# Strassen products for the second matrix product of two SwiGLU FFNs, with weight sums built in DRAM

## The chip, the cores and the metric

The kernel runs on one core of one Trainium2 chip. The metric is the device time of one execution in microseconds; several executions are timed and the median is given. A separate profiled execution supplies the trace. In the profile, PE is TensorE (PEld its weight loads), DVE is VectorE, ACT is ScalarE, POOL is GpSimd, and SP is SyncE, whose queue issues all DMAs of the kernel before.

## What is computed

One decoder layer in float32 on 512 tokens of width 1024. Four sublayers, each followed by a residual addition and a layer normalisation; the first and the last sublayer are SwiGLU FFNs with an inner width of 2816:

```python
def _swiglu(h, w_in, w_out):
    gate, up = jnp.split(h @ w_in, 2, axis=-1)
    return (jax.nn.silu(gate) * up) @ w_out

h = _layernorm(ALPHA * h + 0.5 * _swiglu(h, w_ffn1_in, w_ffn1_out), ln1_g, ln1_b)
h = _layernorm(ALPHA * h + _parallel_mixer(...), ln2_g, ln2_b)
h = _layernorm(ALPHA * h + _memory_attention(...), ln3_g, ln3_b)
h = _layernorm(ALPHA * h + 0.5 * _swiglu(h, w_ffn2_in, w_ffn2_out), ln4_g, ln4_b)
```

The change concerns the second product, `(silu(gate) * up) @ w_out`: 512 x 2816 times 2816 x 1024.

## The kernel before

All operands of the large matmuls are kept as two parts, a rounded high part and the rest (`split`, L64: a cast on ScalarE at L65, a subtraction on VectorE at L66). Each product of two 128-row tiles is three matmuls: high x high, high x low, low x high.

The code is written for a scheduler that fixes the order on each engine when the kernel is built, by operand readiness and by the order of the program, and inserts the semaphores. On the chip each engine then works through its own list in order: an instruction that waits holds up everything behind it on that engine. Buffers come from pools: `b8` has 13 slots of 8 KB a partition; `raw4` has 7 for weights as they arrive (512 KB a load); `q4` has 7 for their split parts. PSUM has 6 banks `mm` and 2 `tr`. A load is issued only when a raw buffer is free, that is when VectorE and ScalarE have read what stood in it.

*First product of an FFN* (`ffn`, L269). It yields the gated activations `gt`, six tiles that hold 22 blocks j of 128 inner columns, transposed. Blocks 0 and 1 are computed directly; the other 20 go two at a time through a Strassen-Winograd scheme: seven products (`a11`, `a12`, `s1`, `s2`, `s3`, `s4`, `a22`) of 12 matmuls of 256 columns each. For each j there is a load of the gate weights (`raw_f1g`, `raw_f2g`) and one of the up weights (`raw_f1u`, `raw_f2u`), both at L277. The sums of weights are made by VectorE at L301 to L304, beginning with `a21 - a22` at L301, which needs the up load. The loop at L367 runs over pairs `gi` = 0, 2, ... 18: products `s1` of the pair, `a22` of the pair before, `s4` and `s2` of the pair, the beginnings (`a12`, `a11`) of a later block, `s3` of the pair, another beginning. L336 subtracts the `s2` product from the gate; with that the PSUM bank of `s2` is read for the last time.

*Second product* (`out_gemm`, L193). For each of two halves of the 1024 output columns it runs over 11 weight blocks, each of 256 contraction rows x 512 columns (`wblock`, L69: a load at L71 and a split). For each block there are four row tiles t, two contraction tiles j and three matmuls of 512 columns:

```python
for i in range(head):
    w = wblock(wsrc[hf, order[i]], f"{name}{hf}_{i}")
    for t in range(NT):
        part(t, i, w)
```

The last blocks of a half (two in the first half, four in the second) are kept and run tile by tile, so that the addition into the residual `h[t]` (L227), the statistics (L230), the normalisation (`ln_tile`, L158) and, in the first FFN, the transposes of a row tile lie beside the matmuls of the next. The activations are split two contraction tiles at a time when they are first used (`act`, L389; 11 splits of 1024 elements).

Of the kernel before, what the change touches and what calls it, by code (L numbers as in the profile page):

```python
# [9 lines left out]
F32 = mybir.dt.float32  # L10
F32R = mybir.dt.float32r
I32 = mybir.dt.int32
AF = mybir.ActivationFunctionType
ALU = mybir.AluOpType
AX = mybir.AxisListType

P = 128
S = 512
D = 1024
KT = D // P  # L20
NT = S // P
FF = 2816
FT = FF // P
# [3 lines left out]
ALPHA = 2.0 ** 0.25  # L27
LN_EPS = 1e-5
# [5 lines left out]
def layer_kernel(ctx: ExitStack, tc: tile.TileContext, a, out):  # L34
    nc = tc.nc
# [3 lines left out]
    res = ctx.enter_context(tc.tile_pool(name="res", bufs=1))  # L39
    sm = ctx.enter_context(tc.tile_pool(name="sm", bufs=6))  # L40
    st = ctx.enter_context(tc.tile_pool(name="st", bufs=4))
    psum = ctx.enter_context(tc.tile_pool(name="psum", bufs=6, space=bass.MemoryType.PSUM))

    def b8(shape, dt, name):
        return big.tile(shape, dt, tag="b8", name=name)

    def mm_ps(name):
        return psum.tile([P, 512], F32, tag="mm", name=name)
# [15 lines left out]
    def split(src, hi, lo):  # L64
        nc.scalar.copy(out=hi, in_=src)  # L65
        nc.vector.tensor_tensor(out=lo, in0=src, in1=hi.bitcast(F32), op=ALU.subtract)  # L66


    def wblock(src, name, stay=False):  # L69
        raw = raw4([P, 1024], f"raw_{name}")  # L70
        nc.sync.dma_start(raw, src)  # L71
        if stay:
            both = b8([P, 2, 1024], F32R, f"ws_{name}")
            hi, lo = both[:, 0, :], both[:, 1, :]
        else:
            hi, lo = q4([P, 1024], f"whi_{name}"), q4([P, 1024], f"wlo_{name}")
        split(raw, hi, lo)
        return hi, lo
# [19 lines left out]
    for k in range(KT):  # L98
        x = xf[k // 4][:, k % 4, :]
# [3 lines left out]
        q = q4([P, 2, 512], f"qx{k}")  # L103
# [9 lines left out]
    def quarters_of(xT):  # L113

        return {n: [(x[:, sl], y[:, sl]) for x, y in xT[k0:k0 + 4]]
                for n, k0, sl in (("b11", 0, lo_), ("b21", 4, lo_), ("b22", 4, hi_))}
# [32 lines left out]
    h = [res.tile([P, D], F32, name=f"h{t}") for t in range(NT)]  # L149


    def ln_bcast(g, b):
        G, B = raw4([P, D], "G"), raw4([P, D], "B")
        nc.sync.dma_start(G, g.partition_broadcast(P))
        nc.sync.dma_start(B, b.partition_broadcast(P))
        return G, B

    def ln_tile(t, stats, GB, eps):  # L158
        G, B = GB
        mv = st.tile([P, 2], F32, tag="mv", name="mv")  # L160
# [32 lines left out]
    def out_gemm(wsrc, nkt, act, alpha, g, b, eps, name, final=False, order=None, stay=4, ys=None, pre=None):  # L193
        nb = nkt // 2
        order = list(range(nb)) if order is None else order
        tiles = None
        stats = [st.tile([P, 2, 6], F32, tag=f"stats{t}", name=f"stats{t}", bufs=1) for t in range(NT)]
        for hf in range(2):
            ps = [None] * NT
            head = nb - (2 if hf == 0 else stay)  # L200

            def part(t, i, w):
                if ps[t] is None:
                    ps[t] = mm_ps(f"{name}ps{hf}{t}")
                hi, lo = w
                for j in range(2):
                    ah, al = act(order[i] * 2 + j)
                    tsl = slice(t * P, (t + 1) * P)
                    wh, wl = hi[:, j * 512:(j + 1) * 512], lo[:, j * 512:(j + 1) * 512]
                    nc.tensor.matmul(ps[t], ah[:, tsl], wh, start=i == 0 and j == 0, stop=False)  # L210
                    nc.tensor.matmul(ps[t], ah[:, tsl], wl, start=False, stop=False)  # L211
                    nc.tensor.matmul(ps[t], al[:, tsl], wh, start=False, stop=i == nb - 1 and j == 1)  # L212
# [5 lines that stand above are left out]
            ws = [wblock(wsrc[hf, order[i]], f"{name}{hf}_{i}", stay=hf == 1 and i < head + 3) for i in range(head, nb)]  # L218
            if hf == 1:
                GB = ln_bcast(g, b)  # L220
                if pre is not None:
                    pre()
            for t in range(NT):
                for i, w in enumerate(ws):
                    part(t, head + i, w)
                sl = slice(hf * 512, hf * 512 + 512)
                nc.vector.scalar_tensor_tensor(  # L227
                    out=h[t][:, sl], in0=h[t][:, sl], scalar=float(alpha), in1=ps[t],
                    op0=ALU.mult, op1=ALU.add)
                nc.vector.bn_stats(stats[t][:, hf, :], h[t][:, sl])  # L230
                if hf == 1:
                    ln_tile(t, stats[t], GB, eps)
                    if final:
                        for q in range(2):
                            nc.sync.dma_start(out[t * P:(t + 1) * P, q * 512:(q + 1) * 512], h[t][:, q * 512:(q + 1) * 512])
                    else:
                        if t == 0:
                            tiles = [b8([P, 2, 2, S], F32R, f"{name}T{q}") for q in range(4)]
                        transpose_h(t, tiles, ys)
        if final:  # L240
            return None
        return [(tiles[k // 2][:, k % 2, 0, :], tiles[k // 2][:, k % 2, 1, :]) for k in range(KT)]


    def proj_T(w, X, n=S, name="pj"):
        hi, lo = w
        ps = mm_ps(name)
        for k in range(KT):
            wsl = slice(k * P, (k + 1) * P)
            mm3(ps[:, :n], hi[:, wsl], lo[:, wsl], X[k][0], X[k][1], k == 0, k == KT - 1)  # L250
        return ps[:, :n]
# [17 lines left out]
    def ffn(win, wout, xT, todo, g, b, name, final, first=None, lead=2, pre=None, ws0=None):  # L269
        gt = [b8([P, 4, S], F32, f"{name}g{q}") for q in range(-(-FT // 4))]  # L270
        raws, quads, ps, sg, c22 = {}, {}, {}, {}, {}
        X = quarters_of(xT)

        def load(j, u):
            if (j, u) not in raws:
                raws[j, u] = raw4([P, 1024], f"raw_{name}{'gu'[u]}{j}")
                nc.sync.dma_start(raws[j, u], win[u * FT + j])  # L277

        def quad(j, p):

# [25 lines left out]
        lo, hi = slice(0, 256), slice(256, 512)  # L306
# [49 lines left out]
        def begin(most):  # L356

            if len(begun) < len(order) and len(begun) - len(ended) < most:
                j = order[len(begun)]
                begun.append(j)  # L360
                product(j, "a12")
                product(j, "a11")
# [4 lines left out]
        for gi in range(0, len(order), 2):  # L367
            two = order[gi:gi + 2]
            for j in two:
                product(j, "s1")  # L370
            for j in order[max(gi - 2, 0):gi]:
                product(j, "a22")
                ended.append(j)
            for p in ("s4", "s2"):
                for j in two:
                    product(j, p)
            begin(4)
            for j in two:
                product(j, "s3")
            begin(4)  # L380
            if not final and 4 <= gi < 4 + 2 * NT:
                t = gi // 2 - 2
                nc.sync.dma_start(h[t], a["x"][t * P:(t + 1) * P, :])
        for j in order[-2:]:
            product(j, "a22")

        gs = {}

        def act(k):  # L389
            if k // 2 not in gs:  # L390
                T = gs[k // 2] = b8([P, 2, 2, S], F32R, f"{name}gs{k // 2}")
                split(gt[k // 4][:, k % 4:k % 4 + 2, :], T[:, :, 0, :], T[:, :, 1, :])
            T = gs[k // 2]
            return T[:, k % 2, 0, :], T[:, k % 2, 1, :]

        return out_gemm(wout, FT, act, 2.0 * ALPHA, g, b, 4.0 * LN_EPS, name, final, pre=pre)


    FQ, FF_, FG, FV = 0, 4, 8, 12
# [39 lines left out]
    for hd in range(H):  # L439
        pf = pf01[hd] if hd < 2 else proj_T(wblock(a["wmix"][FF_ + hd], f"wf{hd}"), X1, name="pf")  # L440
        sl = slice(hd * S, (hd + 1) * S)
# [11 lines left out]
    for hd in range(H):  # L453
        ps = tr_ps("dg")
# [366 lines left out]
```

## Time and profile before

| | |
|---|---|
| median of 3 runs | 1080.48 us (1080.31 to 1081.1) |
| profiled execution | 1082.22 us, of which the span of the trace is 1080.3 us |
| granted TensorE clock | 0.996 |
| busy: PE / VectorE / ScalarE / GpSimd | 1066.6 / 732.4 / 456.2 / 40.2 us |
| moved by DMA | 113.87 MB |
| first FFN: end of its first product | about 231 us |
| last FFN: first product, second product | about 732 to 953 us, 953 to 1073 us |

How to read rows of the profile: a group row gives line, engine, operation, output<-inputs with the shapes and a count, then the busy time of the group and the mean time of one in ns, then idle time of the engine before them and what ended it. A wait row gives who waited for whom, total us, times and longest. A timeline row begins with the start in us and a duration. A windows row gives a stretch, its length, busy time and count for PE, PEld, DVE, ACT and POOL, then the clock, the DMA share and GB/s.

### The profile page before, as it was taken

What the parts mean: (1) busy time and instruction counts of PE and PEld (TensorE: products, weight loads), DVE (VectorE), ACT (ScalarE), POOL (GpSimd) and SP (SyncE); (2) the same over time, 40 slices, a digit from 0 to 9 for tenths busy, and PEclk for the clock granted to TensorE, in tenths of its full rate; (3) what the DMA queues carried; (4) which work ended last, traced back from release to release, by engine and by line L of the source; (5) the groups of instructions that cost most, each with busy time, mean ns of one, the idle gap of its engine ahead of it and who ended that gap; (6) DMA issues with size and microseconds to landing.
All of it is one profiled execution on the core that took longest, in us unless ns stands there. A gap on an engine that the chain in (4) does not pass through costs nothing. (4 is left out here: it accounts for less than half of the span.)

```text
span 1080.3 us, 17019 instructions
## 1 busy us (share of the span) xinstructions
PE 1066.6 (99%) x6758; PEld 966.0 (89%) x6758; DVE 732.4 (68%) x1316; ACT 456.2 (42%) x810; POOL 40.2 (4%) x54
## 2 busy tenths in 40 slices
PE   9999999999999999999999999999999999999997
PEld 8899999998888888889889988888999999988885
DVE  7999878884425733675777456589987888882516
ACT  5666555572221332223415344335555555561300
POOL 0000000000000020411000000010000000000001
PEclk9999999999999999999999999999999999999999
DMA  9243233263341322222415521301323323443302
GB/s 359 72 136 100 89 111 114 80 188 105 106 139 56 99 62 91 71 80 79 156 39 195 153 82 40 128 29 59 118 79 118 118 79 117 135 124 98 133 1 78
DMA packets 34495, 113.87 MB, mean 105 GB/s; under 512 B 4336, under 2 KB 5616, under 8 KB 34416
## 3 DMA queue, kind: packets, MB, share of 16 engines
q1 hardware_dynamic: 34416, 112.78, 32.3%
q8 instruction: 53, 0.87, 0.3%
q14 instruction: 26, 0.21, 0.1%
HBM read 110.67 MB, written 2.10 MB: 104 GB/s over the span
## 5 line engine op out<-in xcount | busy, mean ns | idle before, releaser
L66 DVE TENSOR_TENSOR wlo_f<-raw_f,whi_f 128x1024 fp32r<-128x1024 f32 x38 | 46.5, 1223 | 85.7 <-PE f1ps L211 39.9
L65 ACT CAST whi_f<-raw_f 128x1024 fp32r<-128x1024 f32 x38 | 40.0, 1052 | 103.1 <-PE f2ps L212 46.5
L322 PE MATMUL f2u<-xt,qf2s 128*128 128x256 f32 x480 | 61.8, 284 | 0.7 <-DVE f2sg L336 0.7
L322 PE MATMUL f1u<-xt,qf1s 128*128 128x256 f32 x480 | 61.5, 284 | 0.0
L322 PEld LDWEIGHTS f2u<-xt,qf2s 128*128 128x128 f32 x480 | 59.1, 192 | 1.9 <-issue 1.9
L322 PEld LDWEIGHTS f1u<-xt,qf1s 128*128 128x128 f32 x480 | 59.4, 193 | 0.4 <-ACT qf1s L65 0.4
L210 PE MATMUL f1ps<-whi_f,f1gs 128*128 128x512 f32 x152 | 59.3, 390 | 0.0
L211 PE MATMUL f1ps<-wlo_f,f1gs 128*128 128x512 f32 x152 | 59.2, 389 | 0.0
L211 PE MATMUL f2ps<-wlo_f,f2gs 128*128 128x512 f32 x152 | 59.2, 389 | 0.0
L210 PE MATMUL f2ps<-whi_f,f2gs 128*128 128x512 f32 x152 | 59.1, 389 | 0.0
L212 PE MATMUL f1ps<-whi_f,f1gs 128*128 128x512 f32 x152 | 59.0, 391 | 0.0
L212 PE MATMUL f2ps<-whi_f,f2gs 128*128 128x512 f32 x152 | 58.8, 390 | 0.0
L165 POOL TENSOR_TENSOR rstd<-ve,mhalf 128x1 f32<-128x1 f32 x16 | 14.4, 900 | 685.4 <-DVE ve L163 685.4
L322 PE MATMUL f1v<-xT,qf1s 128*128 128x256 f32 x240 | 32.2, 291 | 2.1 <-ACT qf1s L65 2.1
L212 PEld LDWEIGHTS f2ps<-whi_f,f2gs 128*128 128x128 f32 x152 | 28.5, 188 | 6.1 <-DVE f2gs L66 0.3
L212 PEld LDWEIGHTS f1ps<-whi_f,f1gs 128*128 128x128 f32 x152 | 28.5, 188 | 6.0 <-DVE f1gs L66 0.3
L211 PEld LDWEIGHTS f2ps<-wlo_f,f2gs 128*128 128x128 f32 x152 | 28.5, 188 | 6.0
L210 PEld LDWEIGHTS f2ps<-whi_f,f2gs 128*128 128x128 f32 x152 | 28.5, 188 | 5.9
L211 PEld LDWEIGHTS f1ps<-wlo_f,f1gs 128*128 128x128 f32 x152 | 28.5, 188 | 5.9
L210 PEld LDWEIGHTS f1ps<-whi_f,f1gs 128*128 128x128 f32 x152 | 28.5, 188 | 5.8
L322 PEld LDWEIGHTS f1v<-xT,qf1s 128*128 128x128 f32 x240 | 30.8, 199 | 2.5 <-ACT qf1s L65 2.3
L322 PE MATMUL f1u<-xT,qf1a 128*128 128x256 f32 x240 | 32.1, 283 | 0.0
(337 smaller groups left out, 2957.1 us busy)
## 6 DMA issues: line engine op xcount, KB each, us to landing
raw_f<-in_w1out SPq DMA_DIRECT2D x22, 512.0 KB, 3.9
raw_f2g<-in_w2in SPq DMA_DIRECT2D x22, 512.0 KB, 3.8
raw_f2u<-in_w2in SPq DMA_DIRECT2D x22, 512.0 KB, 4.1
raw_f<-in_w2out SPq DMA_DIRECT2D x22, 512.0 KB, 3.7
raw_f1g<-in_w1in SPq DMA_DIRECT2D x20, 512.0 KB, 4.1
raw_f1u<-in_w1in SPq DMA_DIRECT2D x20, 512.0 KB, 4.4
raw_wk<-in_wk SPq DMA_DIRECT2D x8, 512.0 KB, 4.6
raw_mo<-in_wmixo SPq DMA_DIRECT2D x8, 512.0 KB, 3.6
```

Source lines behind the costliest of these rows:

```text
L65: nc.scalar.copy(out=hi, in_=src)
L66: nc.vector.tensor_tensor(out=lo, in0=src, in1=hi.bitcast(F32), op=ALU.subtract)
L165: nc.gpsimd.tensor_tensor(out=rstd, in0=ve, in1=mhalf[:, 0:1], op=ALU.pow)
L210: nc.tensor.matmul(ps[t], ah[:, tsl], wh, start=i == 0 and j == 0, stop=False)
L211: nc.tensor.matmul(ps[t], ah[:, tsl], wl, start=False, stop=False)
L212: nc.tensor.matmul(ps[t], al[:, tsl], wh, start=False, stop=i == nb - 1 and j == 1)
L322: nc.tensor.matmul(o, q[:, w, wsl], x[k][r], start=opens and k == 0 and n == 0, stop=ends and k == 3 and n == 2, skip_group_check=True)
```

## The change

Of the 22 contraction tiles of the second product, 16 (2048 rows) now go through one level of Strassen-Winograd; the other six go on as plain matmuls, tile by tile, at the end. The activations are cut into quarters `a11`, `a12`, `a21`, `a22` (256 tokens x 1024 inner columns), the weights into four quarters of 1024 rows x 512 columns. Seven products of 4 weight blocks x 2 x 2 x 3 matmuls of 512 columns replace eight. Left sums (`combine`) are made by VectorE in place in `gt`; left operands are split by `left`, two splits of 1024 elements a product; right operands are three quarters as they stand and four sums `t1` to `t4`. PSUM results are added into `h` by VectorE (`add`), eight additions during the Strassen part.

The sums `t1` to `t4` are built in DRAM during the first product of the same FFN. In the loop over pairs, from `gi` = 2 on, four copies of 512 KB from weight to scratch are issued on SP's queue, behind the up load of the pair's second block. With the fourth copy of a set, four accumulating DMAs are put on POOL's queue: t1 and t3 each add one weight block, t2 then adds t1, and t4 adds t2; each waits for what it reads and writes. Sixteen copies make four sets an FFN, at `gi` = 2, 4, 6 and 8. The new parts, cut to the core:

```diff
+    scr = ctx.enter_context(tc.tile_pool(name="scr", bufs=1, space=bass.MemoryType.DRAM))
...
+            for b in range(4):
+                for p, hf, kb in (("t1", 0, b), ("t3", 1, b), ("t2", 1, b + 4), ("t4", 0, b + 4)):
+                    self.todo.append((p, b, hf, kb))
...
+            for p, b, hf, kb in self.todo[:n]:
+                T = self.T[p, b] = scr.tile([P, 1024], F32, name=f"{self.name}{p}{b}")
+                with tc.issue_after(behind):
+                    nc.sync.dma_start(T, self.w[hf, kb])
+                if p == "t4":
+                    for o, x in (("t1", self.w[1, b]), ("t3", self.w[1, b + 4]), ("t2", self.T["t1", b]), ("t4", self.T["t2", b])):
+                        nc.gpsimd.dma_start(self.T[o, b], x, accum_op=ALU.add, max_dma_last_dim=8192)
+            del self.todo[:n]
...
+        u, v, w = ([mm_ps(f"{name}{n}{t}") for t in range(2)] for n in "uvw")
+        L = left("a11")
+        quarter_["s1"] = [x for x in [b8([P, 2, 4, 256], F32, f"{name}s1")] for x in (x[:, 0], x[:, 1])]
+        product(L, "b11", u, True, False)
+        combine("s1", "a21", "a22", ALU.subtract)
+        L = left("s1")
+        for t in range(2):
+            add(t, 0, u[t], True)
+        product(L, "t1", v, True, False)
+        combine("a21", "a11", "a21", ALU.subtract)
+        combine("a11", "s1", "a11", ALU.subtract)
...
+        product(L, "t2", u, False, False)
...
+        product(L, "b21", w, True, False)
+        combine("a12", "a12", "a11", ALU.add)
+        L = left("a21")
...
+        product(L, "t3", u, False, False)
...
+        product(L, "b22", v, False, False)
+        L = left("a22")
+        product(L, "t4", u, False, False)
+        ws = [[wblock(wsrc[hf, kb], f"{name}{hf}_{kb}", stay=hf == 0 or kb < 10) for kb in range(8, FT // 2)]
+              for hf in range(2)]
...
             begin(4)
+            if gi >= 2:
+                sums_out.copy(4, loads[two[-1]])
...
-        return out_gemm(wout, FT, act, 2.0 * ALPHA, g, b, 4.0 * LN_EPS, name, final, pre=pre)
+        return strassen_gemm(wout, gt, sums_out, 2.0 * ALPHA, g, b, 4.0 * LN_EPS, name, final, pre)
```

`product`, inside the new `strassen_gemm`, loads and splits four weight blocks (`right`, through `wblock`) and runs, for each, two contraction tiles x two row tiles x three matmuls into two PSUM banks:

```python
for i, (wh, wl) in enumerate(right(p)):
    for j in range(2):
        for t in range(2):
            for n, (x, y) in enumerate(((ah, wh), (ah, wl), (al, wh))):
                nc.tensor.matmul(ps[t], x, y[:, csl], ...)
```

The tail runs over the four row tiles; for each it takes both column halves with three blocks of weights each, then adds, takes statistics and normalises as before.

More of the change, by code (lines that the diff above doesn't have):

```diff
@@ L242, in out_gemm, with __init__, copy @@
         return [(tiles[k // 2][:, k % 2, 0, :], tiles[k // 2][:, k % 2, 1, :]) for k in range(KT)]
+    class Sums:
+        def __init__(self, wsrc, name):
+            self.w, self.name, self.T, self.todo = wsrc, name, {}, []
+            for b in range(4):
+                for p, hf, kb in (("t1", 0, b), ("t3", 1, b), ("t2", 1, b + 4), ("t4", 0, b + 4)):
+                    self.todo.append((p, b, hf, kb))
+        def copy(self, n, behind):
+            for p, b, hf, kb in self.todo[:n]:
[6 more added lines that the diff above has]
+            del self.todo[:n]
@@ new lines, in strassen_gemm, with left, combine, right @@
+    def strassen_gemm(wsrc, gt, S_, alpha, g, b, eps, name, final, pre):
+        tiles = None
+        stats = [st.tile([P, 2, 6], F32, tag=f"stats{t}", name=f"stats{t}", bufs=1) for t in range(NT)]
+        lo, hi = slice(0, 256), slice(256, 512)
+        quarter_ = {"a11": [gt[0][:, :, lo], gt[1][:, :, lo]], "a12": [gt[2][:, :, lo], gt[3][:, :, lo]],
+                    "a21": [gt[0][:, :, hi], gt[1][:, :, hi]], "a22": [gt[2][:, :, hi], gt[3][:, :, hi]]}
+        def left(p):
+            T = []
+            for i in range(2):
+                t = b8([P, 4, 2, 256], F32R, f"{name}{p}{i}")
+                split(quarter_[p][i], t[:, :, 0, :], t[:, :, 1, :])
+                T.append(t)
+            return T
+        def combine(o, x, y, op):
+            for i in range(2):
+                nc.vector.tensor_tensor(out=quarter_[o][i], in0=quarter_[x][i], in1=quarter_[y][i], op=op)
+        def right(p):
+            direct = {"b11": (0, 0), "b21": (0, 4), "b22": (1, 4)}
+            for i in range(4):
+                src = wsrc[direct[p][0], direct[p][1] + i] if p in direct else S_.T[p, i]
+                yield wblock(src, f"{name}{p}{i}")
+        def product(T, p, ps, opens, ends):
+            for i, (wh, wl) in enumerate(right(p)):
+                for j in range(2):
+                    k = 2 * i + j
+                    csl = slice(j * 512, (j + 1) * 512)
+                    for t in range(2):
+                        tsl = slice(t * P, (t + 1) * P)
+                        ah, al = T[k // 4][:, k % 4, 0, tsl], T[k // 4][:, k % 4, 1, tsl]
+                        for n, (x, y) in enumerate(((ah, wh), (ah, wl), (al, wh))):
+                            nc.tensor.matmul(ps[t], x, y[:, csl], start=opens and k == 0 and n == 0,
+                                             stop=ends and k == 7 and n == 2, skip_group_check=True)
+        def add(t, hf, ps, scale, op=ALU.add):
+            sl = slice(hf * 512, hf * 512 + 512)
+            if scale:
+                nc.vector.scalar_tensor_tensor(out=h[t][:, sl], in0=h[t][:, sl], scalar=float(alpha), in1=ps,
+                                               op0=ALU.mult, op1=op)
+            else:
+                nc.vector.tensor_tensor(out=h[t][:, sl], in0=h[t][:, sl], in1=ps, op=op)
+        u, v, w = ([mm_ps(f"{name}{n}{t}") for t in range(2)] for n in "uvw")
[4 more added lines that the diff above has]
+        L = left("s1")
+        for t in range(2):
+            add(t, 0, u[t], True)
+        product(L, "t1", v, True, False)
+        combine("a21", "a11", "a21", ALU.subtract)
+        combine("a11", "s1", "a11", ALU.subtract)
+        L = left("a11")
+        for t in range(2):
+            add(2 + t, 1, v[t], True)
+        product(L, "t2", u, False, False)
+        L = left("a12")
+        for t in range(2):
+            add(t, 1, u[t], True, ALU.subtract)
+        product(L, "b21", w, True, False)
+        combine("a12", "a12", "a11", ALU.add)
+        L = left("a21")
+        gs = {}
+        for k in range(16, FT, 2):
+            T = gs[k // 2] = b8([P, 2, 2, S], F32R, f"{name}gs{k // 2}")
+            split(gt[k // 4][:, k % 4:k % 4 + 2, :], T[:, :, 0, :], T[:, :, 1, :])
+        product(L, "t3", u, False, False)
+        L = left("a12")
+        for t in range(2):
+            add(2 + t, 1, u[t], False, ALU.subtract)
+        product(L, "b22", v, False, False)
[3 more added lines that the diff above has]
+              for hf in range(2)]
+        GB = ln_bcast(g, b)
+        if pre is not None:
+            pre()
+        for t in range(NT):
+            tsl = slice(t * P, (t + 1) * P)
+            for hf in range(2):
+                if t < 2:
+                    ps = (w, v)[hf][t]
+                else:
+                    ps = u[t - 2] if hf == 0 else mm_ps(f"{name}x{t}")
+                for i, (wh, wl) in enumerate(ws[hf]):
+                    for j in range(2):
+                        csl = slice(j * 512, (j + 1) * 512)
+                        ah, al = gs[8 + i][:, j, 0, tsl], gs[8 + i][:, j, 1, tsl]
+                        for n, (x, y) in enumerate(((ah, wh), (ah, wl), (al, wh))):
+                            nc.tensor.matmul(ps, x, y[:, csl], start=t >= 2 and hf == 1 and i == 0 and j == 0 and n == 0,
+                                             stop=i == 2 and j == 1 and n == 2, skip_group_check=True)
+                add(t, hf, ps, t >= 2 and hf == 0)
+                nc.vector.bn_stats(stats[t][:, hf, :], h[t][:, hf * 512:hf * 512 + 512])
+            ln_tile(t, stats[t], GB, eps)
+            if final:
+                for q in range(2):
+                    nc.sync.dma_start(out[t * P:(t + 1) * P, q * 512:(q + 1) * 512], h[t][:, q * 512:(q + 1) * 512])
+            else:
+                if t == 0:
+                    tiles = [b8([P, 2, 2, S], F32R, f"{name}T{q}") for q in range(4)]
+                transpose_h(t, tiles)
+        if final:
+            return None
+        return [(tiles[k // 2][:, k % 2, 0, :], tiles[k // 2][:, k % 2, 1, :]) for k in range(KT)]
@@ L271, in ffn @@
         raws, quads, ps, sg, c22 = {}, {}, {}, {}, {}
+        loads = {}
+        sums_out = Sums(wout, name)
         X = quarters_of(xT)
@@ L276, in load @@
                 raws[j, u] = raw4([P, 1024], f"raw_{name}{'gu'[u]}{j}")
-                nc.sync.dma_start(raws[j, u], win[u * FT + j])
+                loads[j] = nc.sync.dma_start(raws[j, u], win[u * FT + j]).ins
         def quad(j, p):
@@ L385, in ffn @@
             product(j, "a22")
[L387 to L394, printed above, removed]
-        return out_gemm(wout, FT, act, 2.0 * ALPHA, g, b, 4.0 * LN_EPS, name, final, pre=pre)
+        return strassen_gemm(wout, gt, sums_out, 2.0 * ALPHA, g, b, 4.0 * LN_EPS, name, final, pre)
     FQ, FF_, FG, FV = 0, 4, 8, 12
```

## The prediction

> **What bounds the kernel now.** I read the head of the page first (who is busy), then the DMA line, then windows over the stages that the change touches, then the waits.
>
> ```profile
> span 1080.3 us, 17019 instructions
> PE 1066.6 (99%) x6758; PEld 966.0 (89%) x6758; DVE 732.4 (68%) x1316; ACT 456.2 (42%) x810; POOL 40.2 (4%) x54
> GB/s 359 72 136 100 89 111 114 80 188 105 106 139 56 99 62 91 71 80 79 156 39 195 153 82 40 128 29 59 118 79 118 118 79 117 135 124 98 133 1 78
> ```
>
> PE is busy for all but 14 us, and most of those lie at the two ends. So matmuls that go away shorten the kernel, as long as nothing else becomes the last to arrive. The next fence is one answer of windows: the second product of the last FFN (953 to 1072), a stretch of its first product, and one of the first FFN's first product. The last columns are clock, DMA share and GB/s.
>
> ```profile
> 953.00:1072.00 119.00, 119.00 (x526) 98.32 (x525) 54.30 (x64) 28.23 (x29) 2.41 (x3) 1.00 0.24 76
> 774.00:794.00 20.00, 20.00 (x169) 20.00 (x169) 16.61 (x31) 11.31 (x23) 0.00 (x0) 1.00 0.34 107
> 82.00:102.00 20.00, 20.00 (x169) 20.00 (x168) 17.84 (x35) 12.31 (x24) 0.00 (x0) 1.00 0.34 106
> ```
>
> In the second product PE is never idle, at 119.00/526 = 0.226 us a matmul (512 columns); VectorE is used 46%, ScalarE 24%. In the first product VectorE is at 83 to 89%, and there it also waits for loads:
>
> ```profile
> DVE f2s L301 <- DMA raw_f2u<-in_w2in: 26.3, 16, 3.2
> DVE f1s L301 <- DMA raw_f1u<-in_w1in: 17.5, 13, 2.4
> PE f2u L322 <- DVE f2sg L336: 0.7, 2, 0.4
> ```
>
> VectorE loses 26.3 and 17.5 us to the loads of the second weight half ("up", u), and PE already loses 0.7 us because VectorE frees a PSUM bank late (L336). This stage has little room, and it is where the change puts its DMAs.
>
> **The change, part by part.** (1) *Matmuls.* Before, the 16 contraction tiles take 16 x 4 row tiles x 2 halves x 3 = 384 matmuls; after, 7 products x 4 blocks x 2 x 2 x 3 = 336, with the same 128x128 and 512-column shape. 48 fewer in each FFN, at 0.226 us: 10.85 us, 21.7 us for both. The six other tiles keep their 144.
>
> (2) *VectorE and ScalarE in the second product.* One subtraction of 1024 elements and one cast each:
>
> ```profile
> L66 DVE TENSOR_TENSOR f2gs<-f2g,f2gs 128x1024 fp32r<-128x1024 f32 x11 | 12.7, 1220 | 0.0
> L65 ACT CAST whi_f<-raw_f 128x1024 fp32r<-128x1024 f32 x38 | 40.0, 1052 | 103.1 <-PE f2ps L212 46.5 <-PE f1ps L212 46.3 <-issue 9.6
> L227 DVE SCALAR_TENSOR_TENSOR h<-h,f2ps 128x512 f32<-128x512 f32 x8 | 5.5, 686 | 19.8 <-PE f2ps L212 19.8
> ```
>
> VectorE gets 34 weight blocks to split in place of 22, 17 activation splits in place of 11, 8 sums of quarters (1024 elements, same form as the row above) and 8 more additions into h. That is 12 + 6 + 8 = 26 at 1.15 us (12.7/11, pipelined) = 30 us, plus 8 x 0.69 = 5.5 us: 54.3 + 35.5 = 90 us in a product that shrinks to about 108 us, 83%. The seven Strassen products alone: 28 + 14 + 8 + 3 of 1.15 us and 8 of 0.69 = 66.5 us, with 6 blocks of the rest in advance 73.4, beside 336 x 0.226 = 75.9 us of PE: 97%, of which some 3.5 us (first splits) fall before the first matmul. ScalarE has 51 casts of 1.05: 54 us. PE thus stays the longest, but barely. Price: from 0 (VectorE at 86% in the first product stalls PE for under 1 us) to about 10 us for each FFN (all the gain gone). I take 1.5 us each, 3 us together, since the first product is the nearest row. Behind the last matmul nothing changes: the same addition, statistics and normalisation.
>
> (3) *Loads of the second product.* 34 x 512 KB in 108 us instead of 22 in 119: 0.24 x (34/22) x (119/108) = 0.41 of the DMA engines. Cost nothing, covered by seven raw buffers; 16 of them read sums in DRAM that must be there.
>
> (4) *Copies and accumulations.* Each FFN gets 16 copies from DRAM to DRAM on SP's queue and 16 accumulations on POOL's, 512 KB each, in four sets. Set by set they follow the u loads of tiles 5, 7, 9 and 11. Here is SP's queue there, and what a DMA takes (KB, us to landing):
>
> ```profile
> 789.44 7.02 SPq L277 DMA_DIRECT2D raw_f2u<-in_w2in  x2
> 797.34 12.65 SPq L277 DMA_DIRECT2D raw_f2g<-in_w2in  x2
> 811.05 5.90 SPq L277 DMA_DIRECT2D raw_f2u<-in_w2in  x2
> 94.02 3.76 SPq L277 DMA_DIRECT2D raw_f1u<-in_w1in  x2
> 113.37 5.83 SPq L277 DMA_DIRECT2D raw_f1u<-in_w1in  x2
> raw_f2u<-in_w2in SPq DMA_DIRECT2D x22, 512.0 KB, 4.1
> h<-in_x SPq DMA_DIRECT2D x4, 512.0 KB, 10.8
> out<-h SPq DMA_DIRECT2D x8, 256.0 KB, 2.0
> L277 SPq DMA_DIRECT2D raw_f2g<-in_w2in x9: 328/328/328, 775.7 to 859.6; - x9
> ```
>
> Issuing a copy costs SP 0.33 us, where SP waits for buffers anyway. A period of two tiles is 20.16 us of PE (168 matmuls of 0.12), with four loads: 0.34 x 20.16 / 4 = 1.7 us of all engines for 512 KB. By the page's best slice (359 GB/s) it is 1.46 us. Writing to DRAM is no slower than reading (out lands in 2.0 us). So a set's four copies need about 6 us. An accumulation reads both operands: between one and two times a load, 1.7 to 3.4 us. A period's DMA work becomes 6 + 6 + 6 to 13 = 18 to 25 us of 20.16: full or nearly. The sums have time: the fourth set is issued near 817, its first reader stands at 953 + 11 = 964. POOL has nothing else in this stretch but a memset that sits in its queue until a buffer comes free:
>
> ```profile
> POOL pl L493 <- DVE qf1s L66: 213.5, 2, 212.0
> ```
>
> Were accumulations queued behind it, they would still end before the first FFN's second sub-product, some 240.
>
> What counts is whether a transfer meets a load that is waited for. The gate loads (g) at 797.34 stand behind the copies and land some 6 us later. An earlier one, of 775.66, is cast only at 795.40:
>
> ```profile
> 775.66 12.59 SPq L277 DMA_DIRECT2D raw_f2g<-in_w2in  x2
> 795.40 0.62 ACT L65 CAST qf2a<-raw_f2g 128x512 fp32r<-128x512 f32 x1
> ```
>
> With 4 us to land, 15 us are spare, so these cost nothing. The u loads are the ones without room:
>
> ```profile
> 794.81 0.69 DVE L301 TENSOR_TENSOR f2s<-raw_f2u 128x512 f32<-128x512 f32 x1 [2.06 <-DMA raw_f2u<-in_w2in]
> 799.91 0.69 DVE L301 TENSOR_TENSOR f2s<-raw_f2u 128x512 f32<-128x512 f32 x1 [1.06 <-DMA raw_f2u<-in_w2in]
> 782.53 0.42 DVE L336 TENSOR_TENSOR f2sg<-f2sg,f2u 128x256 f32<-128x256 f32 x1
> 786.29 3.04 PE L322 MATMUL f2u<-xt,qf2s 128*128 128x256 f32 x24
> 804.46 0.41 DVE L336 TENSOR_TENSOR f2sg<-f2sg,f2u 128x256 f32<-128x256 f32 x1
> 806.45 3.04 PE L322 MATMUL f2u<-xt,qf2s 128*128 128x256 f32 x24
> 106.46 0.41 DVE L336 TENSOR_TENSOR f1sg<-f1sg,f1u 128x256 f32<-128x256 f32 x1
> 110.22 3.04 PE L322 MATMUL f1u<-xt,qf1s 128*128 128x256 f32 x24
> ```
>
> VectorE's queue stands at L301 until the u load lands; L336, which frees the bank for PE, is behind it. L336 ends 3.3 us before PE needs it at 786, 1.6 us at 806, and PE waits for it by 888. VectorE's loop, from u load to u load, is thus longer than PE's 20.16 (789.44 to 811.05 is 21.6). So in the last FFN a delay of d at each of 8 u loads costs 8d. In the first FFN the loop is 19.35 (94.02 to 113.37), 0.8 us a period to spare over four periods, and L336 is 3.35 us early at 110, of which I count 2.4: 8d - 5.6, not below 0.
>
> d lies between 0 (never together) and 3.4 us (a whole accumulation in front of each). Copies issued at 796.5 are done by about 804, before the u loads of 811. Accumulations follow one another in the chain t1, t2, t4, each 1.7 to 3.4 of transfer and 2.4 of landing (4.1 - 1.7): about 800 to 818. So the u loads of 811.05 and 816.62 each meet one for part of their transfer. I take d = 1 us: 8 us in the last FFN, 2.4 us in the first.
>
> The Trainium skill's page "Collectives: The Full Stack", section "The bandwidth ceiling: the fold count and why AG ≠ RS ≠ AR", says that an add in the DMA path runs at half a copy's rate, since both operands are read through one ring. By that the accumulation stands at the upper end above, and a sum with d = 2 would give 29 - 21.7 = 8 us slower in place of the gain below; no run here shows an accumulating DMA yet.
>
> **Sum.** -21.7 + 3 (VectorE) + 8 + 2.4 (late u loads) = -8.3 us. The profiled execution took 1082.2 us (span 1080.3); it would become 1073.9. The median of the runs is 1080.5, 1.7 below: I predict 1072.2.
>
> **Rivals.** *The DMAs stay hidden* (d from 0 to 0.3): cost 3 to 5.4 us, time 1062 to 1064. For it: engines are two thirds idle and only part of each u load can meet an accumulation. Against: the work of a period fills it. *The DMA engines are saturated, slower than before* (place: L301 in the first products): accumulations at 3.4 us run into the next set's copies, and every u load waits for one. With d = 2.5: 20 + 14.4 + 3 - 21.7 = +15.7, 1096. The sum is zero where 16d - 5.6 + 3 = 21.7, at d = 1.5; above that the change loses. For it: 18 to 25 us of work in 20.16, and two PSUM waits that exist already. Against: the copies are issued right after the u loads, not before them. Beside this stands the Trainium skill's "DMA: Bandwidth & Descriptors", section "Issuing engines are not separate DMA queues": issuing from POOL gives no other engines, all interleave on the same 16. That agrees with this rival's mechanism; of POOL's queue this trace has no DMA to show. *VectorE becomes the bound of the second product*: 97% use with waits at each sum of quarters costs 5 us a FFN, 10 in place of 3: 1079, no change. *The saving does not appear* because the remaining matmuls run slower: excluded, they have the same shape and a new 128x128 weight load each, as now (PEld 98 of 119 us).
>
> **How the numbers follow.** My case (d from 0.4 to 1.4, 1065 to 1079): 0.41. Hidden: 0.21. Saturated: 0.26. VectorE bound: 0.12. About 0.2% (2.2 us) is what a measurement of this kernel can tell from no change. Faster: 0.38 of the first, all of the hidden case and a little of the last, 0.60. Same: 0.12. Slower: 0.28, the saturated case and what VectorE adds if both come. The range of 8 in 10 goes from 1060 (d = 0, VectorE nearly free) to 1094 (d about 2.4); the first case's own range is 1065 to 1079.
>
> **What would show it.** Right: 480 matmuls in place of 528 between the last L322 and the last normalisation of each FFN, in some 110 us without PE gaps over 1 us; the waits of L301 for u loads up by 5 to 10 us in each FFN; PE waiting for L336 for some 8 us in the last FFN's first product and little in the first's; u loads of tiles 6 to 13 landing about 1 us later than 4.1. Wrong: u loads landing in 6 us or more, PE waits for L336 over 15 us (saturated); no new wait there (hidden); or PE waiting in the second product for weight or activation splits of L66 (VectorE bound). The prediction is also wrong if SP itself stands behind the copies, so that u loads are issued late rather than land late.

## The result, and the profile after

The changed kernel took 1095.49 us in the median of four runs (1091.77 to 1098.38), beside 1080.79 us for the kernel before: 1.0133 times as long, 95% interval 1.0100 to 1.0166. It is slower by 14.7 us, where 8.3 us less were forecast. The profiled execution was the fastest of the four, 1091.77 us, with a span of 1090.0 us, so it shows 9.7 us of the loss.

From the page of the changed kernel: the head, the granted clock and the DMA share in 40 slices, and the two queues with their packets, MB and share of 16 engines.

```profile
span 1090.0 us, 17139 instructions
PE 1055.6 (97%) x6662; PEld 957.1 (88%) x6662; DVE 799.5 (73%) x1384; ACT 490.4 (45%) x846; POOL 65.8 (6%) x86
PEclk9999999999999999999999999999998899999999
DMA  9599823345680322212416421412998433256622
q1 hardware_dynamic: 38896, 142.15, 38.8%
q0 software_dynamic: 2560, 16.78, 8.2%
```

The 96 matmuls are gone (6758 to 6662) and PE has 11 us less to do, yet it is busy 97% instead of 99%. In the slices of the two first products (the first nine, and slices 28 to 36) the DMA row reaches 8 and 9, and two slices of PEclk read 8.

Windows over the four stages show where the time went: first and second product of the first FFN, then of the last FFN. The columns are the stretch, its length, busy time of PE, weight loads, VectorE, ScalarE and POOL, then clock, DMA share and GB/s. A first product is counted from the first L322 matmul of its Strassen part to the last, so blocks 0 and 1 lie ahead of it; in the first FFN of before it ends at 234.2 us, not near 231. First the kernel before, then the changed one:

```profile
27.80:234.20 206.40, 204.31 (x1682) 203.45 (x1682) 177.31 (x326) 120.59 (x228) 0.53 (x6) 0.99 0.34 110
234.20:357.20 123.00, 122.99 (x555) 101.36 (x554) 60.25 (x76) 35.39 (x43) 2.94 (x3) 1.00 0.31 97
748.80:953.00 204.20, 203.49 (x1682) 202.21 (x1682) 170.86 (x316) 113.69 (x221) 0.00 (x0) 1.00 0.34 109
953.00:1072.80 119.80, 119.79 (x528) 98.65 (x526) 54.30 (x64) 28.23 (x29) 2.41 (x3) 1.00 0.24 78
```

```profile
26.80:244.70 217.90, 209.18 (x1682) 206.83 (x1682) 176.91 (x326) 119.57 (x228) 13.17 (x22) 0.98 0.61 184
244.70:358.40 113.70, 112.79 (x507) 92.25 (x506) 94.90 (x113) 53.20 (x62) 2.96 (x3) 1.00 0.49 160
750.20:972.50 222.30, 209.51 (x1682) 208.75 (x1682) 170.58 (x316) 113.73 (x221) 12.53 (x16) 0.96 0.60 176
972.50:1082.50 110.00, 109.19 (x481) 89.73 (x479) 88.25 (x99) 45.90 (x47) 2.77 (x3) 1.00 0.44 144
```

The second products became 9.3 and 9.8 us shorter. The first products, with the same 1682 matmuls, became 11.5 and 18.1 us longer. That is +29.6 - 19.1 = +10.5 us, and 0.8 us less elsewhere makes the 9.7. The growth has two parts. PE's idle time (length minus busy) rose from 2.1 to 8.7 and from 0.7 to 12.8 us, 18.7 in sum; its busy time for the same matmuls rose by 4.9 and 6.0 us, 10.9 in sum, at a clock of 0.98 and 0.96. The second part is told with the hardware below.

The waits of the changed kernel (us in total, times, longest) and its DMA issues over the whole span (count, KB each, median us to landing):

```profile
DVE f2s L436 <- DMA raw_f2u<-in_w2in: 44.5, 16, 8.3
DVE f1s L436 <- DMA raw_f1u<-in_w1in: 31.5, 15, 6.0
L457 PE MATMUL f2u<-xt,qf2s 128*128 128x256 f32 x480 | 67.3, 301 | 12.8 <-DVE f2sg L471 11.1
L457 PE MATMUL f1u<-xt,qf1s 128*128 128x256 f32 x480 | 65.4, 293 | 6.7 <-DVE f1sg L471 6.0
f2t<-in_w2out SPq DMA_DIRECT2D x16, 512.0 KB, 8.3
f2t<-in_w2out POOLq DMA_DIRECT2D x8, 512.0 KB, 8.6
f2t<-f2t POOLq DMA_DIRECT2D x8, 512.0 KB, 7.6
```

L436, L457 and L471 are L301, L322 and L336 of before. VectorE waits for the u loads 44.5 and 31.5 us, where it was 26.3 and 17.5, and PE in turn waits for VectorE's L471 11.1 and 6.0 us, where it was 0.7 in the last FFN. The next fence has the same DMA view for the four periods of the last FFN alone (785 to 868 us): the DMA share in 40 slices and the u loads, first before, then after, and last the u loads of the first FFN (70 to 145 us), before and after.

```profile
DMA  0185028500006813840000771294000068119400
raw_f2u<-in_w2in SPq DMA_DIRECT2D x8, 512.0 KB, 4.1
DMA  9999999579999998999266999699989805991000
raw_f2u<-in_w2in SPq DMA_DIRECT2D x6, 512.0 KB, 6.8
raw_f1u<-in_w1in SPq DMA_DIRECT2D x8, 512.0 KB, 4.3
raw_f1u<-in_w1in SPq DMA_DIRECT2D x7, 512.0 KB, 6.3
```

The engines had pauses before and have almost none after. The u loads land 2.7 and 2.0 us later in the median.

One set from issue to end, from the timelines of SP, POOL, VectorE and PE (start us, length, engine, line, operation, count, idle time before it and what ended it):

```profile
802.58 2.61 SPq L259 DMA_DIRECT2D f2t<-in_w2out  x4
811.54 0.77 POOL L262 DMA_DIRECT2D f2t<-in_w2out  x1 [8.05 <-DMA f2t<-in_w2out]
815.84 12.28 SPq L412 DMA_DIRECT2D raw_f2u<-in_w2in  x2
826.47 0.69 DVE L436 TENSOR_TENSOR f2s<-raw_f2u 128x512 f32<-128x512 f32 x1 [8.34 <-DMA raw_f2u<-in_w2in]
826.67 0.78 POOL L262 DMA_DIRECT2D f2t<-f2t  x1 [7.05 <-DMA f2t<-f2t]
838.59 5.46 PE L457 MATMUL f2u<-xt,qf2s 128*128 128x256 f32 x24 [5.00 <-DVE f2sg L471]
```

Four copies go out from 802.58, the first accumulations at 811.54, the last at 826.67; that one lands 5.5 us later, at 832.2. The set takes some 30 us, longer than the 20 us period, and the last accumulation of the set before it goes out at 802.72, beside these copies. The u load issued at 815.84 in the midst of it starts VectorE only at 826.47, 10.6 us later, and PE then stands 5.00 us until 838.59.

### The profile page after: what moved, and what is told of

Same layout as the page of the kernel before. It is cut to its first block, busy times and chain, and to the rows that moved or that the text cites. A ratio compares the mean times of both kernels' runs of the same rounds, so it can differ in the third digit from the quotient of the medians.

```text
span 1090.0 us, 17139 instructions
## 1 busy us (share of the span) xinstructions
PE 1055.6 (97%) x6662; PEld 957.1 (88%) x6662; DVE 799.5 (73%) x1384; ACT 490.4 (45%) x846; POOL 65.8 (6%) x86
## 3 DMA queue, kind: packets, MB, share of 16 engines
q1 hardware_dynamic: 38896, 142.15, 38.8%
## 5 line engine op out<-in xcount | busy, mean ns | idle before, releaser
L457 PE MATMUL f2u<-xt,qf2s 128*128 128x256 f32 x480 | 67.3, 301 | 12.8 <-DVE f2sg L471 11.1
L457 PEld LDWEIGHTS f2u<-xt,qf2s 128*128 128x128 f32 x480 | 65.0, 210 | 13.5 <-issue 11.6
L457 PE MATMUL f1u<-xt,qf1s 128*128 128x256 f32 x480 | 65.4, 293 | 6.7 <-DVE f1sg L471 6.0
L457 PEld LDWEIGHTS f1u<-xt,qf1s 128*128 128x128 f32 x480 | 62.0, 200 | 8.6 <-issue 7.2
L436 DVE TENSOR_TENSOR f2s<-raw_f2u 128x512 f32<-128x512 f32 x20 | 13.8, 691 | 44.6 <-DMA raw_f2u<-in_w2in 44.5
L436 DVE TENSOR_TENSOR f1s<-raw_f1u 128x512 f32<-128x512 f32 x20 | 13.7, 691 | 31.5 <-DMA raw_f1u<-in_w1in 31.5
L457 PE MATMUL f1v<-xT,qf1s 128*128 128x256 f32 x240 | 32.2, 291 | 2.1 <-ACT qf1s L66 2.1
L457 PEld LDWEIGHTS f1v<-xT,qf1s 128*128 128x128 f32 x240 | 31.0, 200 | 2.5 <-ACT qf1s L66 2.3
L457 PE MATMUL f2w<-xoT,qf2a 128*128 128x256 f32 x240 | 32.8, 287 | 0.0
L457 PE MATMUL f1w<-xT,qf1a 128*128 128x256 f32 x240 | 32.2, 284 | 0.0
L457 PE MATMUL f2u<-xoT,qf2a 128*128 128x256 f32 x240 | 32.0, 283 | 0.0
L457 PE MATMUL f1u<-xT,qf1a 128*128 128x256 f32 x240 | 32.0, 283 | 0.0
L457 PEld LDWEIGHTS f2w<-xoT,qf2a 128*128 128x128 f32 x240 | 31.2, 197 | 0.1
L457 PEld LDWEIGHTS f1w<-xT,qf1a 128*128 128x128 f32 x240 | 30.6, 193 | 0.1
L67 DVE TENSOR_TENSOR wlo_wv<-raw_wv,whi_wv 128x1024 fp32r<-128x1024 f32 x12 | 14.7, 1224 | 21.5 <-PE vps L603 12.6
L457 PE MATMUL f1u<-xt,qf1a 128*128 128x256 f32 x240 | 30.4, 283 | 0.0
L457 PE MATMUL f2v<-xt,qf2s 128*128 128x256 f32 x240 | 30.4, 283 | 0.0
L457 PE MATMUL f2v<-xoT,qf2s 128*128 128x256 f32 x240 | 30.4, 283 | 0.0
L457 PE MATMUL f2u<-xt,qf2a 128*128 128x256 f32 x240 | 30.4, 283 | 0.0
L457 PE MATMUL f1v<-xt,qf1s 128*128 128x256 f32 x240 | 30.4, 283 | 0.0
L457 PEld LDWEIGHTS f1u<-xT,qf1a 128*128 128x128 f32 x240 | 30.2, 192 | 0.0
```

The lines of the kernel that those rows point to most:

```text
L436: nc.vector.tensor_tensor(out=s1, in0=a21, in1=a22, op=ALU.subtract)
L457: nc.tensor.matmul(o, q[:, w, wsl], x[k][r], start=opens and k == 0 and n == 0, stop=ends and k == 3 and n == 2, skip_group_check=True)
```

## The experiments

The theory: the accumulating DMAs fill the 16 engines, the u loads land late, VectorE stops at L436 and PE at the bank that L471 frees. The rivals: the copies, not the accumulations; instructions, waits and queue order, not bytes; or the second product itself.

**e1: Strassen with no sums at all.** Copies and accumulations are left out, and the operands of t1 to t4 are plain weight blocks, as many loads as before.

```diff
...
-            if gi >= 2:
-                sums_out.copy(4, loads[two[-1]])
```

> Strassen second products without any copy or accumulation; their right operands t1 to t4 are plain weight blocks, so the sums of weights are left out. Theory A (the DMA engines are full in four periods of each first product, so loads of up weights land late): first products return to the 206 and 204 us of before, second products stay at 114 and 110 us, time near 1080.8 - 9.3 - 9.9 = 1061.6. Theory B (the new order of instructions, not the DMAs, makes the first products longer): they stay at about 218 and 222 us, time near 1093. Theory C (Strassen itself stalls VectorE): second products over 115 us.

1061.73 us, 0.9834 of before (0.9816 to 0.9851). Its stages, the first product of the first FFN, then the first and second product of the last:

```profile
27.91:234.27 206.36, 204.27 (x1682) 203.45 (x1681) 177.31 (x326) 120.44 (x228) 0.53 (x6) 0.99 0.35 111
739.60:941.79 202.19, 202.19 (x1682) 201.91 (x1681) 170.94 (x316) 114.01 (x221) 0.00 (x0) 1.00 0.34 110
941.60:1051.70 110.10, 109.32 (x482) 89.86 (x480) 88.31 (x98) 46.07 (x47) 2.41 (x3) 1.00 0.45 145
```

The second product is as long as in the changed kernel (110.1 and 110.0 us), and the loss of both first products is gone (206.4 and 202.2 us, beside 206.4 and 204.2 before). So the second product isn't to blame: Strassen there is worth 18.5 us, and making the sums costs 33.8 us.

**e2: the copies alone.** No accumulation is issued; the operands are the bare copies.

```diff
-                if p == "t4":
-                    for o, x in (("t1", self.w[1, b]), ...):
-                        nc.gpsimd.dma_start(self.T[o, b], x, accum_op=ALU.add, ...)
```

> The 16 copies of each FFN stay, the 16 accumulations go (the sums of weights are left out, the products read the copies). Theory A with the work of both kinds counting: DMA share of the four periods about 0.33 + 4.4/20 = 0.55, up loads at 4 to 5 us, first products within 3 us of before, time 1062 to 1068. Theory A2 (the copies, which are long and stand in the queue of the loads, do the harm): first products stay over 212 us each, time over 1080.

1061.31 us, 0.9827 (0.9812 to 0.9843), the same as e1. A stretch of its first product, then its waits:

```profile
774.00:794.00 20.00, 20.00 (x169) 20.00 (x168) 16.17 (x30) 10.76 (x21) 0.00 (x0) 1.00 0.53 183
DVE f2s L433 <- DMA raw_f2u<-in_w2in: 25.3, 17, 3.0
```

Sixteen more DMAs of 512 KB in each FFN cost nothing that can be seen, and in this trace each set of them has landed before the next pair of u loads is issued. The DMA share rises to 0.53; VectorE's waits for u loads in the last FFN are as before, in the first FFN 20.2 us beside 17.5.

**e3: plain copies in place of the accumulations.** Same queue, same waits, same bytes written, but the second operand isn't added; the sums are left out.

```diff
-  nc.gpsimd.dma_start(self.T[o, b], x, accum_op=ALU.add, max_dma_last_dim=8192)
+  nc.gpsimd.dma_start(self.T[o, b], x, max_dma_last_dim=8192)
```

> The accumulations become plain copies on the same queue, with the same waits, descriptors and destinations, and without the second read (the sums are left out). If the bytes read twice are what fills the engines (accumulation about 2.8 us of all engines against 1.1 of a copy): DMA share of the periods falls from 0.98 to about 0.75, the first products lose a half or more of their extra 11.5 and 18.2 us, time 1068 to 1080. If any DMA from POOL's queue disturbs the loads as much: time within 5 us of the changed kernel, 1090 or more.

1073.09 us, 0.9935 (0.9915 to 0.9955), 11.8 us above e2 and 22.4 below the changed kernel. Its POOL queue (packets, MB, share), a landing and a wait:

```profile
q0 software_dynamic: 2560, 16.78, 4.7%
f2t<-f2t POOLq DMA_DIRECT2D x8, 512.0 KB, 4.8
DVE f2s L436 <- DMA raw_f2u<-in_w2in: 35.7, 16, 4.6
```

Plain copies at the place of the accumulations cost 11.8 us, and the adding makes it 34. The first products, 210.6 and 211.8 us, lose 7.3 and 10.5 of their extra 11.5 and 18.1 us, as the theory of the bytes read twice expected. Engine time per DMA from the shares: 8.2% of 1090.0 us over 32 accumulations is 2.79 us of all 16 engines each; 4.7% of 1072.8 us over 32 plain copies is 1.58 us. An accumulation is 1.77 copies of its own queue. Copies on SP's queue are cheaper: between e1 and e2, which differ only in the copies and in where the loads read, q1 goes from 36.4% of 1059.1 us to 40.0% of 1059.8, which is 1.2 us for each of 32, and by that an accumulation is 2.3. The two queues cut a copy differently, into 80 packets on POOL's and 32 on SP's; whether that is the reason isn't shown.

**e4: the same instructions with hardly any bytes.** Each copy and accumulation covers 8 of 128 rows; the operands are plain blocks, as in e1.

```diff
...
-  nc.sync.dma_start(T, self.w[hf, kb])
+  nc.sync.dma_start(T[:8], self.w[hf, kb][:8])
-  nc.gpsimd.dma_start(self.T[o, b], x, accum_op=ALU.add, max_dma_last_dim=8192)
+  nc.gpsimd.dma_start(self.T[o, b][:8], x[:8], accum_op=ALU.add, max_dma_last_dim=8192)
...
```

> All 32 copies and 32 accumulations stay with their waits and places, each cut to 8 of 128 rows (32 KB in place of 512); the products read plain weight blocks, the sums are left out. Theory A (bytes on the engines): as without sums, 1061 to 1064, L436 waits near 26 and 18 us. Theory B (issue times on SP, waits on POOL, changed order): first products over 212 us, time over 1080.

1061.40 us, 0.9827 (0.9807 to 0.9846): e1 again. Issues, semaphores, SP's order and POOL's queue cost nothing that can be seen. All of the cost is transfers. Whether the DMA engines themselves are what is full, or the DRAM behind them, no run separates.

The next four compute everything. Either it counts how full a period is, so that the same work over twice as many periods would hide (A1), or where an accumulation falls beside the u loads (A2).

**e5: the last FFN's sums made earlier**, in the attention stage, copies behind its weight loads; the first FFN's as in the changed kernel.

```diff
...
+    sums2 = Sums(a["w2out"], "f2")
...
+            sums2.copy(1, last[0])    # behind each wv load
...
+        sums2.copy(2, last[0])        # behind each pair of wq loads
```

> The last FFN's 16 copies and 16 accumulations move to the memory attention, one or two copies behind each load of the value and query weights; the first FFN as in the changed kernel. Theory A (accumulations that run beside the up loads of a first product make them late): last FFN's first product back from 222 to 203 or 204 us, its second product 110 us, first FFN's first product still 216 to 218 us; time 1095.5 - 20 = 1072 to 1077. Rival (the attention stage has no more room than the first products): the attention grows by 5 us or more, time 1080 or more.

1076.68 us, 0.9958 (0.9934 to 0.9982). First products of the first and the last FFN:

```profile
27.13:250.39 223.26, 209.90 (x1682) 207.72 (x1681) 176.82 (x326) 119.77 (x228) 13.17 (x22) 0.97 0.60 179
755.41:959.34 203.93, 203.50 (x1682) 202.18 (x1681) 170.96 (x316) 113.85 (x221) 0.00 (x0) 1.00 0.34 109
```

The last FFN's first product is whole again (203.9 us), and what is left stands in the first FFN, whose 223.3 us lie above the 216 to 218 expected; this traced execution took 1078.57 us, 1.9 above the median. Between the two first products lie 505.0 us, and 505.5 in the changed kernel, so the attention did not grow and the rival falls.

**e6: two copies and two accumulations per step in place of four and four every second step.** t1 and t3 follow one step's copies; t2 and t4, of which t4 reads t2's result, follow the next step's.

```diff
-  if p == "t4": # all four accumulations
+  if p in ("t3", "t4"): # t1 and t3 with t3's copy, t2 and t4 with t4's
...
-                sums_out.copy(4, loads[two[-1]])
+                sums_out.copy(2, loads[two[-1]])
```

> Both FFNs in place, but two copies a step over eight steps, with t1 and t3 added in one step and t2 and then t4 (a chain) in the next. Theory A1 (total work of the engines: 0.33 + (2 x 1.1 + 2 x 2.8)/20 = 0.72 of a period instead of 0.98): up loads near 5 us, first products 206 to 210 us, time 1063 to 1070. Theory A2 (a single accumulation that meets an up load is enough; the chain of t2 and t4 reaches into the next up loads at every second step): first products 4 to 9 us over before, time 1070 to 1080.

1078.94 us, 0.9991 (0.9973 to 1.0008): no different from before, 16.6 us better than the changed kernel, above the 1063 to 1070 that A1 expected and within the 1070 to 1080 of A2. In the traced execution, 1082.91 us and so 4 us above the median, the first products are 12.2 and 8.1 us over before, where A2 had 4 to 9.

**e9: the same two and two per step, but all t1 and t3 first, then all t2, then all t4**, so that no accumulation waits for one of its own step.

```diff
-  for p, hf, kb in (("t1", 0, b), ("t3", 1, b), ("t2", 1, b + 4), ("t4", 0, b + 4)):
-      self.todo.append((p, b, hf, kb))
+      self.todo += [("t1", b, 0, b), ("t3", b, 1, b)]
+  self.todo += [("t2", b, 1, b + 4) for b in range(4)] + [("t4", b, 0, b + 4) for b in range(4)]
...
```

> As the spread kernel with the same two copies and two accumulations a step, but in an order in which the two of a step are independent (all t1 and t3, then t2, then t4), so that both should land some 5 + 8 us behind the up load that starts them and before the next one, about 15 us later. Theory A1: the same time as the spread kernel within 2 us. Theory A2: 4 to 10 us faster than it, first products within 2 us of before, time 1061 to 1065.

1070.34 us, 0.9901 (0.9886 to 0.9916), between the two theories' numbers. It moves the same bytes through the same queues in the same number of steps as e6 and is 8.6 us faster (1068.08 to 1071.02 beside 1076.87 to 1085.71): how full a period is (A1) doesn't explain that alone. A2's gain of 4 to 10 us came; its 1061 to 1065 did not, nor first products within 2 us of before: they are 3.4 and 5.0 us over. Waits and both first products of e6, then of e9, and three rows of e9:

```profile
DVE f2s L437 <- DMA raw_f2u<-in_w2in: 35.6, 16, 5.8
27.63:246.21 218.58, 208.72 (x1682) 206.76 (x1681) 176.89 (x326) 120.02 (x228) 13.17 (x22) 0.98 0.63 181
751.39:963.72 212.33, 205.50 (x1682) 203.75 (x1681) 170.45 (x316) 113.48 (x221) 12.54 (x16) 0.99 0.64 184
```

```profile
DVE f2s L437 <- DMA raw_f2u<-in_w2in: 32.0, 17, 4.3
27.69:237.48 209.79, 206.05 (x1682) 203.85 (x1681) 176.96 (x326) 120.03 (x228) 13.16 (x22) 0.99 0.66 189
742.53:951.68 209.15, 205.40 (x1682) 203.67 (x1681) 170.40 (x316) 113.60 (x221) 12.54 (x16) 0.99 0.65 187
791.01 1.13 SPq L259 DMA_DIRECT2D f2t<-in_w2out  x2
799.73 0.77 POOL L263 DMA_DIRECT2D f2t<-in_w2out  x1 [0.45 <-issue]
803.98 8.60 SPq L413 DMA_DIRECT2D raw_f2u<-in_w2in  x2
```

In e9 an accumulation still goes out at 799.73, 8.7 us behind its copy, and by the 6.4 us that they take to land in that kernel it is under way when the u load of 803.98 starts.

**e10: e9's order, and the last FFN's sums early as in e5.** No new edit.

> The phased order for the first FFN, and the last FFN's sums built during the memory attention. If the phased order leaves no loss in the last FFN: equal to the phased kernel within 2 us; if the last FFN, whose VectorE loop is the longer, still loses: faster than it by that loss. Time 1060 to 1066.

1065.73 us, 0.9863 (0.9838 to 0.9889), as expected, and the best of all that compute everything: 29.8 us below the changed kernel, 14.5 below the 1080.19 of the kernel before beside it. Its first products:

```profile
27.48:239.29 211.81, 206.03 (x1682) 203.86 (x1681) 176.83 (x326) 120.06 (x228) 13.16 (x22) 0.99 0.66 187
745.05:948.57 203.52, 202.86 (x1682) 201.99 (x1681) 170.83 (x316) 113.70 (x221) 0.00 (x0) 1.00 0.34 109
```

What stays lost against e1 is mostly in the first FFN: 211.8 us there beside 206.4.

## Why the prediction was wrong, point by point

**The step that failed is part 4's choice of d**, the delay of a u load. It was taken as 1 us from a set that would end "about 800 to 818"; it was 2.7 us in the last FFN and 2.0 in the first. Two things were wrong in it. The landing: 2.4 us was added to the transfer as for a load, so 4.1 to 5.8 us for an accumulation, and medians of 7.6 to 9.1 were measured; with copies of 8.3 us in front and a chain of three accumulations (t1, t2, t4) behind, a set became some 30 us long, where the prediction had 21.5. And the engine time: 2.79 us is inside the bounds of 1.7 to 3.4, in their upper half, while the sum went by d = 1 as if at the lower end. The working of a period was too low as well: with its own 1.7 us for each load and copy and 1.7 to 3.4 for an accumulation it is 20.4 to 27.2 us, not 18 to 25, so it was full even at the lower bound. With the measured price (four copies, four loads of 1.7, four accumulations of 2.79) that is 4.4 + 6.8 + 11.2 = 22.4 us of engine time in 20.16. The 1.1 us for a copy is an estimate: q1's time grew from 32.3% of 1080.3 to 38.8% of 1090.0 us, by 74 us; 24 more weight loads at before's 1.62 (349 us over 215 times 512 KB) are 39, and the other 35 are 32 copies; e1 and e2 give 1.2.

**The term's size.** Forecast were 8 + 2.4 us; the first products grew by 18.1 + 11.5. With the measured d the prediction's own formula gives 8 x 2.7 = 21.6 and 8 x 2.0 - 5.6 = 10.4, 32.0 in place of 29.6 measured. This closeness is partly luck: only 18.7 us of it is PE waiting, and 10.9 us is a slower clock, a term that the prediction didn't have.

**The rival that came true** is the saturated one: place (L301, now L436) and mechanism hold, the measured d lies above its break-even of 1.5, and its 1096 at d = 2.5 stands beside 1095.5. It had every u load hit, but the one issued at about 801 us landed in 3.7. What was put forward against it, that copies are issued right behind the u loads, is true of the copies (e2: free) and not of the accumulations, which in the set shown go out 9 to 24 us behind the first copy. Of the marks set for it, u loads landing in 6 us or more were seen (6.8 and 6.3), and PE waits for L471 over 15 us in the sum of both FFNs (17.1).

**What was right.** The saving: 96 matmuls, -21.7 us, less 1.5 and 1.1 us of other loss in the second products (10.85 against 9.3 and 9.8), forecast 1.5 each. In the last FFN's, for which 83% was forecast, VectorE is busy 88.25 of 110.0 us, 80%; it isn't the bound, since PE is idle there for only 0.8 us. The copies (e2) and SP's issue time (e4) cost nothing that can be seen, nor do the loads of the second product, at a DMA share of 0.44 where 0.41 was forecast.

**The rule of half a copy's rate**, from the Trainium skill's page "Collectives: The Full Stack", section "The bandwidth ceiling: the fold count and why AG ≠ RS ≠ AR", by which the prediction worked out 8 us slower at d = 2, is told there of a collective's reduce-scatter beside its all-gather. For this kernel's accumulations e3 and the changed kernel agree with it roughly, 1.77 copies of the same queue in place of 2. It should have weighed more.

**What stays open.** Which u load is hit in which execution: the changed kernel's four runs lie 6.6 us apart, e5's five 7.5 us, and only one execution of each is traced, up to 4 us off the median, so the parts of a stage are known less well than the medians. And the first FFN's 5.4 us in e10, since no experiment moved those sums elsewhere.

## What to carry to other kernels

A DMA that hides by its average share may still stand in front of the one load that is waited for: lay its whole chain, landing times included, over the issue times of that load, and if the chain is longer than the period, as here 30 us against 20, expect it to meet that load. Price an accumulating DMA here at about two copies (1.8 to 2.3), and where one must wait for another, put them in different steps (e9), or in a stage that does not grow by it (e5, e10). A gain in one stage that needs work in another should first be run without that work, as e1: the 18.5 us was real, and what remained was a question of where to put 32 DMAs.

## What the runs showed of the hardware that was not expected

A short wait of PE can halve its clock for a while. Four of PE's steps in the changed kernel, the last undisturbed, with 24 matmuls in 3.04 us, then windows over stretches inside the first and the second (the clock is the third column from the end):

```profile
809.81 4.59 PE L457 MATMUL f2u<-xt,qf2s 128*128 128x256 f32 x24 [1.80 <-DVE f2sg L471]
838.59 5.46 PE L457 MATMUL f2u<-xt,qf2s 128*128 128x256 f32 x24 [5.00 <-DVE f2sg L471]
827.82 2.89 PE L457 MATMUL f2u<-xt,qf2s 128*128 128x256 f32 x22 [1.67 <-DVE qf2s L67]
847.09 3.04 PE L457 MATMUL f2v<-xt,qf2s 128*128 128x256 f32 x24
811.50:813.00 1.50, 1.50 (x9) 1.50 (x9) 1.23 (x3) 1.50 (x4) 0.78 (x2) 0.50 1.12 442
838.60:844.50 5.90, 5.90 (x28) 5.90 (x29) 5.56 (x11) 3.82 (x8) 0.46 (x1) 0.50 0.96 164
```

After 1.80 us of waiting the matmuls ran on at half the clock and took 4.59 us; after 5.00 us, 5.46. The stretch of half clock lasted 3.4 us in some places and 6.8 in others. Not every wait does it: the one of 1.67 us above, one of 2.0 us in e3 and one of 2.5 us in e5 did not. The kernel before has one such stretch too, at 41.3 us, 2 us behind a wait of 2.06; the changed kernel has five more in its first products. PE's busy time there grew by 10.9 us, nearly all of it in these stretches, beside 18.7 us of added waiting. The Trainium skill's page "TensorE: Matmul & The Clock Gate", section "What's actually happening", has free-running windows of about 3.4 us and the half rate after at least one idle window. The lengths agree with these rows; that a wait of 1.80 us, half a window, is enough does not follow from it, and the measurement decides.
